# Two hybrid token-mixer layers in three-product float32r on one core: recurrence gates by blocks of 80 channels, rotated scores as stacked float32r products, another order of steps

## The chip, the cores and the metric

One Trainium2 chip, and of it one NeuronCore. The engines named below are TensorE (PE; PEld is its weight load), VectorE (DVE), ScalarE (ACT), GpSimd (POOL) and the sync engine (SP), which here issues nearly all DMAs. The metric is the time of one execution on the device in microseconds (us). It was measured three times for the kernel before; one more execution was recorded by the hardware profiler, and all rows of a trace come from that one.

## The reference, cut to what matters

Two layers run one after the other on x of 256 tokens by 1024 channels. Each projects the normalised x with one wide matrix and feeds three token mixers, whose outputs are gated, projected, merged and projected back:

```python
for l in range(DEPTH):                                   # DEPTH = 2
    h = rmsnorm(x, pre_norm_g[l])
    u, v, z_a, c_q, c_kv, k_rope, z_b, x_c, z_c, g_a, g_b, g_c = split(h @ w_in[l])
    y_a = gmlp_spatial(u, v, ...) * silu(z_a)            # spatial gating, 1024 channels
    y_b = mla_attention(c_q, c_kv, k_rope, ...) * silu(z_b)   # 8 heads
    y_c = rg_lru(x_c, ...) * silu(z_c)                   # recurrence, 1280 channels
    merged = (sigmoid(g_a) * (y_a @ w_proj_a[l]) + sigmoid(g_b) * (y_b @ w_proj_b[l])
              + sigmoid(g_c) * (y_c @ w_proj_c[l]))
    x = x + rmsnorm(merged @ w_out[l], post_norm_g[l])
```

Two places matter for the change. In the attention a head's score is a product over 128 plain channels plus a product over 64 rotated channels, whose key is shared by all heads. In `rg_lru` the gates come from block-diagonal matrices, 16 blocks of 80 by 80, with a bias:

```python
q, k = concat([q_nope, rope(q_rope)]), concat([k_nope, rope(k_rope)])    # 128 + 64
s = einsum('bqhd,bkhd->bhqk', q, k) * scale
...
xb = xc.reshape(B, S, 16, 80)                            # xc: causal conv of x_c
r = sigmoid(einsum('bshi,hij->bshj', xb, w_a).reshape(B, S, C) + b_a)
i = sigmoid(einsum('bshi,hij->bshj', xb, w_x).reshape(B, S, C) + b_x)
```

## The kernel before, in words

**Products.** A float32 operand is kept as two float32r tiles, a rounded high part (hi) and what is left (lo). `mm3` makes a product out of three matmuls, hi by hi, hi by lo and lo by hi (L307, L308, L309), so a 1024-deep projection onto 256 columns (`ch_mm`, one step of most keys) is 48 matmuls of 128x256. Scores, transposes and the value product of the attention use plain float32 tiles.

**Weights.** Each step of the list ORDER that needs weights has its own chunk, of 1 MB for most. A chunk is loaded by SP into one of three raw buffers (L200; the gates' pieces L210), split by ACT into hi (a copy, L268) and by DVE into lo (a subtraction, L269), and the split lands in one of three hi/lo pairs. When a step is through with its pair it hands it back: `done` puts the pair into the list and `pump` emits the split of the next chunk on ACT and DVE, then the load that the freed raw buffer takes. At which of a step's points that happens is set per key by LATE (`fin`). So ACT's and DVE's queues carry, in program order, a step's own work and the split of a chunk three ahead.

**Order.** Engines work through their instructions in the order in which the program emits them; that order is ORDER, written out by hand and used in both layers: steps for the low-rank queries and keys (xc, turn, conv, uq, ukv), the attention by pairs of heads (attend 0 to 5: scores of pair i, transposes of pair i-1, values of pair i-2), the spatial gating (v, norm, u, za), the merging gates (ga, gb, gc), their projections (pa, pb, pc), the output gates (zb, zc), and the recurrence (conv, split, stack, la, lx, r1, r2, r3).

**PSUM and temporaries.** `bank` is a ring of five PSUM banks (mm in the traces, mm_83 to mm_87 in the order), `aux` a ring of three, `tmp` a ring of eight 128x512 tiles in SBUF (t). A ring is taken in turn, so a step that takes a bank waits for the reader of what lay there five takes ago. Sixteen slots of SBUF hold the larger tiles.

**Recurrence gates.** The 1280 channels are two groups of five tiles of 128. Blocks of 80 cut across tiles of 128, so a gate chunk is 1280 columns of mostly zeros: POOL clears the raw buffer (L205), some 16 to 20 small DMAs lay the pieces (L210), and `lru_gate` multiplies in a mix of forms: 24 matmuls of 256 columns for each key (la, lx) and group, one in six of them with 96 rows (L927). The inputs that straddle tiles are gathered by `conv_stack` with copies on POOL, DVE and ACT (L447 is one of their lines). The bias enters in the sigmoid on ACT (L932), which writes the gates to SBUF, where `recur1` reads them: a multiply on DVE, five exponentials (L942) and five tanh (L944) on ACT, a square on DVE. `recur2` is two passes on DVE (L951, L952) and a square root on ACT (L953), `recur3` the scan.

**Scores.** `scores` makes four float32 products per head: the plain part at 128 and at 256 columns (L728, L730) and the rotated part at 128 and 256 columns (L729, L731). A plain float32 matmul is issued as two instructions (two passes), so the trace counts 32 for 16 heads. krt holds the rotated key twice, in rows 0 to 63 for one head of a pair and in rows 64 to 127 for the other, with zeros in the other half; qr holds a pair's rotated queries one above the other. The queries are rotated in `queries` (key uq): four copies on ACT (L643) and three operations on DVE (L646 is the second).

Of the kernel before, what the change touches and what calls it, by code (L numbers as in the profile page):

```python
# [7 lines left out]
F32 = mybir.dt.float32  # L8
# [5 lines left out]
P = 128  # L14
# [20 lines left out]
R_Q, R_KV, R_LG, R_LB, R_CW, R_CB, R_BA, R_BX, R_LAM, R_N = 0, 3, 5, 13, 21, 61, 71, 81, 91, 101  # L35
# [6 lines left out]
COL_EVEN, COL_ODD, COL_STACK, LRU_N = 0, GT * P, (GT + 2) * P, (GT + 5) * P  # L42


STACKS = ((0, ((1, 0, 32),)), (4, ((3, 96, 32),)), (2, ((1, 96, 32), (3, 0, 16))))
SH = 32
# [5 lines left out]
    ("wl", 0), ("xc", 0), ("turn", 0), ("xc", 1), ("conv", 0), ("uq", 0), ("conv", 1), ("xc", 2), ("ukv", 0),  # L52
    ("conv", 2), ("ukv", 1), ("decay", 0), ("ws", 0), ("xc", 3), ("uq", 1), ("attend", 0), ("shift", 0),
    ("uq", 2), ("v", 0),
    ("attend", 1), ("xc", 4), ("conv", 3), ("v", 1), ("conv", 4), ("uq", 3), ("attend", 2), ("split", 1),
    ("v", 2), ("v", 3), ("attend", 3), ("split", 0), ("norm", 0), ("u", 0), ("stack", 0), ("attend", 4),
# [9 lines left out]
LATE = {"ga": 1, "gb": 1, "lx": 1, "pa": 1, "ukv": 1, "uq": 3, "v": 1, "xc": 1}  # L66


SE = {
# [3 lines left out]
}  # L73

# [20 lines left out]
def tile_trunk(ctx: ExitStack, tc, I, out):  # L95
# [5 lines left out]
    sm = ctx.enter_context(tc.tile_pool(name="sm", bufs=2))  # L101
    psm = ctx.enter_context(tc.tile_pool(name="psm", bufs=1, space=bass.MemoryType.PSUM))
# [65 lines left out]
    for l in range(L):  # L168
# [4 lines left out]
        for key, j in ORDER:  # L173
            if key in COLS:
                c = Chunk(KT, CW, win(l, COLS[key] + j * CW))
            elif key == "uq":
                c = Chunk(3, 384, proj("mla_w_uq", l, 0, 3, j * 384, 384), kind="heads")
            elif key == "ukv":
                c = Chunk(2, 1024, proj("mla_w_ukv", l, 0, 2, j * 1024, 1024))
            elif key in ("la", "lx"):  # L180
                c = Chunk(LRU_N // P, P, lru=("lru_w_" + key[1], l, j))
# [12 lines left out]
    def load(c, parts=1, mid=None):  # L194
# [9 lines left out]
        name, l, g = c.lru  # L204
        G.memset(c.raw[:, :n], 0.0)  # L205

        def piece(row, col, r0, c0, nr, ncol):

            b = r0 // BW
            nc.sync.dma_start(  # L210
                c.raw[row : row + nr, col : col + ncol],
                I[name][l, g * 8 + b, r0 - b * BW : r0 - b * BW + nr, c0 - b * BW : c0 - b * BW + ncol],
            )

        for b in range(8):
            for k in range(GT):
                r0, r1 = max(b * BW, k * P), min(b * BW + BW, k * P + P)
                if r0 < r1 and k % 2 == 0:
                    piece(r0 - k * P, COL_EVEN + b * BW, r0, b * BW, r1 - r0, BW)
                elif r0 < r1:  # L220
                    c0, c1 = max(b * BW, k * P), min(b * BW + BW, k * P + P)
                    piece(r0 - k * P, COL_ODD + k // 2 * P + c0 - k * P, r0, c0, r1 - r0, c1 - c0)
        for n_, (m, runs) in enumerate(STACKS):
            for k, r, nr in runs:
                for b in range(8):
                    r0, r1 = max(b * BW, k * P + r), min(b * BW + BW, k * P + r + nr)
                    c0, c1 = max(b * BW, m * P), min(b * BW + BW, m * P + P)
                    if r0 < r1 and c0 < c1:
                        piece(r0 - k * P - r, COL_STACK + n_ * P + c0 - m * P, r0, c0, r1 - r0, c1 - c0)

    def split(c, parts=1, mid=None):
# [27 lines left out]
        if c.lru:  # L259
            act(hi[:, :n], c.raw[:, :n], AF.Copy)  # L260
            st = slice(COL_STACK, n)
            act(hi[SH : 2 * SH, st], c.raw[:SH, st], AF.Copy)
            V.tensor_tensor(lo[:, :COL_STACK], c.raw[:, :COL_STACK], f(hi[:, :COL_STACK]), ALU.subtract)
            V.tensor_tensor(hi[2 * SH : 3 * SH, st], c.raw[:SH, st], f(hi[:SH, st]), ALU.subtract)
            return
# [190 lines left out]
    with tc.manual_schedule():  # L456
# [10 lines left out]
        for i in range(2):  # L467
            G.memset(krt[i], 0.0)
# [62 lines left out]
        for l in range(L):  # L531
# [62 lines left out]
            def turn_ranks(_):  # L594
                for b in range(3):
# [9 lines left out]
                    for i in range(2):  # L605
# [15 lines left out]
            qr = slot("qr", (4, S))  # L621
# [5 lines left out]
            def queries(j):  # L627
# [68 lines left out]
            def conv_split(g):  # L696
                xh, xl = slot("xh", (GT, S), F32R), slot("xl", (GT, S), F32R)
                split_act(xh, xl, xc[g])
                cv[g] = xc[g], xh, xl

            def conv_stack(g):

                _, xh, xl = cv[g]
                xs, two = slot("xs", (GT, S), F32R), xm
                for src, dst in ((xh, xs[:, 3:5]), (xl, two)):
                    copy(SE.get("wide", "V"), dst[:64], f(src[:64, 2:5:2]))
                    copy(SE.get("wide2", "A"), dst[64:], f(src[64:, 0:3:2]))
                for n, (_, runs) in enumerate(STACKS):
                    for p, src in enumerate((xh, xl, xh)):
                        at = p * SH  # L710
                        for k, r, nr in runs:
                            copy(SE.get(("thin", n, p), "V"), xs[at : at + nr, n], f(src[r : r + nr, k]))
                cv[g] += (xs, two)

            cv = {}
# [397 lines left out]
```

## Time and profile before

| | |
|---|---|
| three executions | 797.0, 799.04, 799.51 us, median 799.04 |
| the profiled execution | 798.34 us, of it 796.6 us span of the trace |
| PE | 788.1 us busy, 99% of the span |
| DVE | 548.9 us, 69% |
| ACT | 469.3 us, 59% |
| POOL | 70.5 us, 9% |
| DMA | 137.87 MB, 173 GB/s on the mean |

The span runs from the first to the last recorded instruction; 1.74 us of the profiled execution lie around it. A group row of the profile reads: line, engine, operation, written tile <- read tiles, shape, count | total us, mean ns of one | idle time of the engine ahead of it and what ended it. Matmul durations in group rows overlap (a matmul is in the pipe for longer than it holds it), so what a matmul costs is read from the distance between starts in the timeline, or from the chain that ended last, whose rows add up to the span.

### The profile page before, as it was taken

What the parts mean: (1) busy time and instruction counts of PE and PEld (TensorE: products, weight loads), DVE (VectorE), ACT (ScalarE), POOL (GpSimd) and SP (SyncE); (2) the same over time, 40 slices, a digit from 0 to 9 for tenths busy, and PEclk for the clock granted to TensorE, in tenths of its full rate; (3) what the DMA queues carried; (4) which work ended last, traced back from release to release, by engine and by line L of the source; (5) the groups of instructions that cost most, each with busy time, mean ns of one, the idle gap of its engine ahead of it and who ended that gap; (6) DMA issues with size and microseconds to landing.
All of it is one profiled execution on the core that took longest, in us unless ns stands there. A gap on an engine that the chain in (4) does not pass through costs nothing.

```text
span 796.6 us, 15355 instructions
## 1 busy us (share of the span) xinstructions
PE 788.1 (99%) x6445; PEld 780.2 (98%) x6445; DVE 548.9 (69%) x712; ACT 469.3 (59%) x689; POOL 70.5 (9%) x110
## 2 busy tenths in 40 slices
PE   9999999999999999999999999999999999999996
PEld 8999999999999999999999999999999999999996
DVE  5587788666876787555666868776578578775562
ACT  5785767339855736343567776654595584544441
POOL 1100503003000000000010032031210000000000
PEclk9999999999999999999999999999999999999998
DMA  7845454344666565666357626541575656564531
GB/s 229 290 152 182 153 161 155 112 122 137 201 213 211 159 215 169 199 212 216 109 171 239 208 94 211 159 128 51 166 219 167 221 162 202 185 214 150 193 132 54
DMA packets 134205, 137.87 MB, mean 173 GB/s; under 512 B 11046, under 2 KB 130808, under 8 KB 134136
## 3 DMA queue, kind: packets, MB, share of 16 engines
q1 hardware_dynamic: 134120, 136.90, 54.3%
q8 instruction: 50, 0.82, 0.4%
q14 instruction: 19, 0.16, 0.1%
q10 hardware_dynamic: 16, 0.00, 0.0%
HBM read 135.83 MB, written 1.05 MB: 172 GB/s over the span
## 4 chain that ended last, share of the span: by engine, by line
PE 94%; DMA 2%; issue 1%; DVE 1%; ACT 1%; SPq 0%; POOL 0%; POOLq 0%; DVEq 0%; ACTq 0%
PE mm L308 25%; PE mm L307 25%; PE mm L309 25%; PE mm L431 2%; PE mm L433 2%; PE mm L432 2%; DMA raw<-in_w_in_dram 1%; PE aux L843 1%; PE mm L730 1%; PE aux L770 1%; PE mm L731 1%; DMA X<-in_x_dram 1%; PE mm L549 1%; PE aux L1021 1%; PE mm L1020 1%
## 5 line engine op out<-in xcount | busy, mean ns | idle before, releaser
L269 DVE TENSOR_TENSOR wlo<-raw,whi 128x2048 fp32r<-128x2048 f32 (+5 forms) x123 | 264.6, 2156 | 115.9 <-ACT whi L268 115.5
L307 PE MATMUL mm<-hT,whi 128*128 128x256 f32 x1088 | 307.1, 282 | 0.0
L309 PE MATMUL mm<-hT,wlo 128*128 128x256 f32 x1088 | 305.8, 281 | 0.3 <-DVE wlo L269 0.3
L308 PE MATMUL mm<-hT,whi 128*128 128x256 f32 x1088 | 305.6, 281 | 0.0
L268 ACT ACTIVATE whi<-raw 128x2048 fp32r<-128x2048 f32 (+5 forms) x123 | 221.0, 1802 | 66.6 <-PE mm L308 26.8
L309 PEld LDWEIGHTS mm<-hT,wlo 128*128 128x128 f32 x1088 | 205.0, 188 | 0.5 <-DVE wlo L269 0.5
L307 PEld LDWEIGHTS mm<-hT,whi 128*128 128x128 f32 x1088 | 205.0, 188 | 0.0
L308 PEld LDWEIGHTS mm<-hT,whi 128*128 128x128 f32 x1088 | 205.0, 188 | 0.0
L973 ACT ACTIVATE t<-mm 128x512 f32<-128x512 f32 x18 | 10.8, 598 | 52.2 <-PE mm L309 52.2
L397 POOL TENSOR_TENSOR rstd<-rstd,mhalf 128x1 f32<-128x1 f32 x8 | 4.4, 551 | 391.1 <-DVE rstd L396 391.1
L308 PE MATMUL mm<-yc,whi 128*128 128x256 f32 x128 | 36.0, 282 | 0.0
L308 PE MATMUL mm<-ya,whi 128*128 128x256 f32 x128 | 36.0, 282 | 0.0
L307 PE MATMUL mm<-ya,whi 128*128 128x256 f32 x128 | 36.0, 281 | 0.0
L307 PE MATMUL mm<-yc,whi 128*128 128x256 f32 x128 | 36.0, 281 | 0.0
L431 PE MATMUL mm<-whi,hT 128*128 128x256 f32 x128 | 36.0, 281 | 0.0
L308 PE MATMUL mm<-yb,whi 128*128 128x256 f32 x128 | 35.9, 281 | 0.0
L309 PE MATMUL mm<-ya,wlo 128*128 128x256 f32 x128 | 35.9, 280 | 0.0
L309 PE MATMUL mm<-yc,wlo 128*128 128x256 f32 x128 | 35.9, 280 | 0.0
L309 PE MATMUL mm<-yb,wlo 128*128 128x256 f32 x128 | 35.8, 280 | 0.0
L307 PE MATMUL mm<-yb,whi 128*128 128x256 f32 x128 | 35.8, 280 | 0.0
L432 PE MATMUL mm<-wlo,hT 128*128 128x256 f32 x128 | 35.8, 279 | 0.0
L433 PE MATMUL mm<-whi,hT 128*128 128x256 f32 x128 | 35.7, 279 | 0.0
(279 smaller groups left out, 1663.4 us busy)
## 6 DMA issues: line engine op xcount, KB each, us to landing
raw<-in_w_in_dram SPq DMA_DIRECT2D x76, 1024.0 KB
raw<-in_w_proj_a_dram SPq DMA_DIRECT2D x8, 1024.0 KB
raw<-in_w_proj_b_dram SPq DMA_DIRECT2D x8, 1024.0 KB
raw<-in_w_proj_c_dram SPq DMA_DIRECT2D x8, 1024.0 KB
raw<-in_w_out_dram SPq DMA_DIRECT2D x8, 1024.0 KB
raw<-in_mla_w_uq_dram SPq DMA_DIRECT2D x8, 576.0 KB
raw<-in_mla_w_ukv_dram SPq DMA_DIRECT2D x4, 1024.0 KB
raw<-in_w_in_dram SPq DMA_DIRECT2D x4, 640.0 KB
```

The source lines that it names most:

```text
L268: act(hi[:, w], c.raw[:, w], AF.Copy)
L269: V.tensor_tensor(lo[:, w], c.raw[:, w], f(hi[:, w]), ALU.subtract)
L307: mm(ps, lh, rh, start=start, stop=False)
L308: mm(ps, lh, rl, start=False, stop=False)
L309: mm(ps, ll, rh, start=False, stop=stop)
L431: mm(ps, lh, rh, start=k == 0, stop=False)
L432: mm(ps, lh, rl, start=False, stop=False)
L433: mm(ps, ll, rh, start=False, stop=k == KT - 1)
L549: mm(ps, ll, rh, start=False, stop=j % 2 * 4 + k == KT - 1)
L730: mm(sc[:, P : 3 * P], qn[:, P:], kn, start=True, stop=False)
L731: mm(sc[:, P : 3 * P], qp[:, P:], kr, start=False, stop=True)
L973: act(sg, ps, AF.Sigmoid)
```

## The change

**Gates by blocks.** A key's chunk is now `lg`, for four blocks (h = 0 to 3) and both gates. The stacked input is 80 hi rows, a row of ones and 47 lo rows (128 deep), and a second one 80 hi rows, one of ones and the other 33 lo rows (114 deep); the stacked weights are hi weights with the bias as row 80, and hi again for the lo rows, against lo weights. So a block needs two matmuls of 256 columns instead of a mix of forms, and a step `lg` is 16 matmuls into four banks with 80 output rows each. Four sigmoids of 80x512 without bias follow, and each result is stored to DRAM (L908 in the new numbering); `gate_in` (key in, L915) reads the gates of a group back in the layout of 128 channels to a tile. The conv output's hi and lo parts go to DRAM too (L687), and `conv_stack` reads them back as blocks (L698, L699), two slots for each h, after POOL has set rows 64 to 95 to one. The clearing of raw buffers, the small pieces, the gathering copies, the bias columns and their transposed rows are gone.

**Scores.** krt and qr become float32r: krt0 is the rotated key's hi part in both halves, krt1 its lo part, and qr holds for every head its hi rows above its lo rows (or below, for the second of a pair). A head's rotated part is two float32r matmuls in one pass each at 128 columns, and two at 256, in place of one float32 matmul (two passes) at each. Every uq step gets two copies on ACT and two subtractions on DVE of 64x256, after its pump.

**Order.** ORDER is another one, and LATE holds `lg` at 1 in place of `lx`.

```diff
 ORDER = (
...
-    ("za", 0), ("u", 1), ("za", 1), ("attend", 5), ("u", 2), ("za", 2), ("u", 3), ("za", 3), ("ga", 0),
-    ("la", 0), ("lx", 0), ("r1", 0), ("stack", 1), ("pa", 0), ("ga", 1), ("pa", 1), ("la", 1), ("r2", 0),
...
+    ("za", 2), ("u", 3), ("stack", 1), ("conv", 4), ("za", 3), ("attend", 5), ("conv", 3), ("lg", 0), ("ga", 0),
+    ("split", 1), ("pa", 0), ("ga", 1), ("lg", 1), ("in", 0), ("pa", 1), ("ga", 2), ("stack", 2), ("pa", 2),
+    ("r1", 0), ("stack", 3), ("ga", 3), ("r2", 0), ("pa", 3), ("zb", 0), ("r3", 0), ("lg", 2), ("zb", 1),
+    ("zb", 2), ("zb", 3), ("lg", 3), ("gb", 0), ("pb", 0), ("in", 1), ("gb", 1), ("pb", 1), ("r1", 1), ("r2", 1),
...
-LATE = {"ga": 1, "gb": 1, "lx": 1, "pa": 1, "ukv": 1, "uq": 3, "v": 1, "xc": 1}
+LATE = {"ga": 1, "gb": 1, "lg": 1, "pa": 1, "ukv": 1, "uq": 3, "v": 1, "xc": 1}
...
-        G.memset(c.raw[:, :n], 0.0)
...
+        l, g = c.lru
+        for i, x in enumerate("ax"):
+            at = slice(i * WH, (i + 1) * WH)
+            w = I["lru_w_" + x][l, g * NH : (g + 1) * NH].rearrange("b r c -> r b c")
+            r1, r2 = v2(c.raw[:, at], BW), v2(c.raw[:, W2 + i * WH : W2 + (i + 1) * WH], BW)
+            nc.sync.dma_start(r1[:BW], w)
+            nc.sync.dma_start(r1[B1:], w[:K1])
+            nc.sync.dma_start(c.raw[BW:B1, at], I["lru_b_" + x][l : l + 1, g * WH : (g + 1) * WH])
+            nc.sync.dma_start(r2[64 : B1 + K2], w[K1 - (B1 - 64) :])
...
-            act(hi[:, :n], c.raw[:, :n], AF.Copy)
...
+            raw, r2 = c.raw[:, :W2], c.raw[64 : B1 + K2, W2 : 2 * W2]
+            act(hi[:, :W2], raw, AF.Copy)
+            act(lo[64 : B1 + K2, :W2], r2, AF.Copy)
+            V.tensor_tensor(lo[:B1, :W2], raw[:B1], f(hi[:B1, :W2]), ALU.subtract)
...
+                for a in range(2):
+                    own, other = (slice(i * HR, (i + 1) * HR) for i in (a, 1 - a))
+                    to = qr[j // 2][:, j % 2 * 2 + a]
+                    act(to[own], qa[own, :S], AF.Copy)
+                    V.tensor_tensor(to[other], qa[own, :S], f(to[own]), ALU.subtract)
...
+                    d = dp.tile([GT * P, S], F32, tag=f"{w}{g}", name=nm(w))
+                    nc.sync.dma_start(d.rearrange("(k p) s -> p k s", p=P), f(x))
...
+            def conv_stack(h):
+                _, _, dh, _, dl = cv[h // 2]
+                rows = slice(h % 2 * WH, (h % 2 + 1) * WH)
+                bh, bl = (d[rows].rearrange("(b r) s -> r b s", r=BW) for d in (dh, dl))
+                st2[h] = [slot("xs", (NH, S), F32R) for _ in range(2)]
+                for x, b in zip(st2[h], (bl[:K1], bl[K1:])):
+                    G.memset(f(x[64:96]), 1.0)
+                    nc.sync.dma_start(f(x[:BW]), bh)
+                    nc.sync.dma_start(f(x[B1 : B1 + b.shape[0]]), b)
...
-                    mm(sc[:, 0:P], qp[:, 0:P], kr[:, 0:P], start=False, stop=True)
...
-                    mm(sc[:, P : 3 * P], qp[:, P:], kr, start=False, stop=True)
...
+                    for o, ts, n in ((sc[:, 0:P], slice(0, P), P), (sc[:, P : 3 * P], slice(P, S), S)):
+                        mm(o, qn[:, ts], kn[:, :n], start=True, stop=False)
+                        mm(o, qp[:, ts], krt[0][:, :n], start=False, stop=False)
+                        mm(o, qp[:, ts], krt[1][:, :n], start=False, stop=True)
...
+            def lru_gates(h):
...
+                    for b0 in range(0, NH, 2):
+                        ps, o = bank(), tmp()
+                        for b in (b0, b0 + 1):
+                            ws = slice(i * WH + b * BW, i * WH + (b + 1) * BW)
+                            pb = ps[:BW, (b - b0) * S : (b - b0 + 1) * S]
+                            mm(pb, wh[:, ws], x1[:, b], start=True, stop=False)
+                            mm(pb, wl[: B1 + K2, ws], x2[: B1 + K2, b], start=False, stop=True)
+                        act(o[:BW], ps[:BW], AF.Sigmoid)
+                        nc.sync.dma_start(rows[:, b0 : b0 + 2], v2(o[:BW], S))
+                fin(c, "lg", 1)
+
+            def gate_in(g):
+                for key in ("la", "lx"):
+                    o = slot(key, (GT, S))
+                    nc.sync.dma_start(o, gates[key, g].rearrange("(k p) s -> p k s", p=P))
+                    gates[key, g] = o
```

The first place is ACT's queue around the step ga 1 of the first layer. In the order of before, whi is a chunk's hi part written by the split, t_80 is ga 1's gate (a sigmoid, L875) and la the recurrence gate of group 1, with its bias from pt:

```order
L260 ACTIVATE whi_92<-raw_89 128x1280
L262 ACTIVATE whi_92<-raw_89 32x384
L268 ACTIVATE whi_94<-raw_90 128x2048
L875 ACT_TABLE_LOAD
L875 ACTIVATE t_80<-mm_84 128x512
L268 ACTIVATE whi_96<-raw_91 128x2048
L932 ACTIVATE la_2268<-mm_81,pt_349 128x256 x2
L932 ACTIVATE la_2268<-mm_82,pt_349 128x256 x2
```

In the changed kernel the same place reads as follows (L243 is the split's copy, L860 the gate's sigmoid, L907 that of the recurrence gates):

```order
L243 ACTIVATE whi_98<-raw_93 128x2048
L243 ACTIVATE whi_94<-raw_91 128x2048
L860 ACTIVATE t_78<-mm_86 128x512
L907 ACTIVATE t_79<-mm_87 80x512
L907 ACTIVATE t_80<-mm_83 80x512
L907 ACTIVATE t_81<-mm_84 80x512
L907 ACTIVATE t_82<-mm_85 80x512
L243 ACTIVATE whi_96<-raw_92 128x2048
```

The step after ga 1 is lg 1 now, not pa 1, and lg 1 takes four banks (mm_87, 83, 84, 85) after the one of ga 1 (mm_86); pa 1, which follows, takes the fifth, mm_86.

The second place is ACT's queue at the recurrence of group 0. Of before (a, la and u are tiles of the recurrence, xs the stacked inputs of group 1):

```order
L942 ACT_TABLE_LOAD
L942 ACTIVATE a_2079<-la_2013,sA_777 128x256 x5
L944 ACTIVATE la_2013<-la_2013,sT_776 128x256 x5
L447 ACTIVATE xs_2093<-xl_1255 32x256 x3
L447 ACTIVATE xs_2093<-xl_1255 16x256
L447 ACTIVATE xs_2093<-xh_1254 32x256
L447 ACTIVATE xs_2093<-xh_1254 16x256
L260 ACTIVATE whi_92<-raw_89 128x1280
```

Of the changed kernel (L923 and L925 are the exponentials and tanh, L934 the root, L954 the sigmoid of zb 0, and t_76 the gate of ga 3):

```order
L923 ACTIVATE a_2351<-la_2176,sA_743 128x256 x5
L925 ACTIVATE la_2176<-la_2176,sT_742 128x256 x5
L237 ACTIVATE whi_98<-raw_93 128x640
L238 ACTIVATE wlo_99<-raw_93 50x640
L860 ACT_TABLE_LOAD
L860 ACTIVATE t_76<-mm_84 128x512
L934 ACT_TABLE_LOAD
L934 ACTIVATE u_2352<-u_2352 128x1280
L243 ACTIVATE whi_94<-raw_91 128x2048
L954 ACT_TABLE_LOAD
L954 ACTIVATE t_77<-mm_86 128x512
```

The root, which stood behind the gates of group 1, now follows the exponentials with one gate of ga 3 between, and the sigmoid of zb 0 stands behind both and behind a split.

The third place is SP's queue at the step ga 1. Of before there are only weights (raw):

```order
L210 DMA raw_91<-in_lru_w_x_dram 16x64 x2
L200 DMA raw_89<-in_w_proj_a_dram 128x8x256
L200 DMA raw_90<-in_w_in_dram 128x8x256
L200 DMA raw_91<-in_w_proj_a_dram 128x8x256
L210 DMA raw_89<-in_lru_w_a_dram 80x80
```

Of the changed kernel (la_1955 and lx_1968 are the gates in DRAM, la_2176 and lx_2178 those in SBUF; L201 to L205 are the pieces of an lg chunk):

```order
L192 DMA raw_91<-in_w_proj_a_dram 128x8x256
L908 DMA la_1955<-t_79 80x2x256
L908 DMA la_1955<-t_80 80x2x256
L908 DMA lx_1968<-t_81 80x2x256
L908 DMA lx_1968<-t_82 80x2x256
L192 DMA raw_92<-in_w_in_dram 128x8x256
L915 DMA la_2176<-la_1955 128x5x256
L915 DMA lx_2178<-lx_1968 128x5x256
L201 DMA raw_93<-in_lru_w_a_dram 80x4x80
```

Stores of the gates, a load of weights, and the reads of the gates now stand in one queue, in this order.

More of the change, by code (lines that the diff above doesn't have):

```diff
@@ L32 @@
 CWID = 4
[L35 to L46, printed above, removed]
+R_Q, R_KV, R_LG, R_LB, R_CW, R_CB, R_LAM, R_N = 0, 3, 5, 13, 21, 61, 71, 81
+NH, K1 = 4, 47
+K2 = BW - K1
+WH = NH * BW
+W2 = 2 * WH
+B1 = BW + 1
 SLOT_W = 1296
 ORDER = (
[L52 to L56, printed above, removed]
[6 rows of a table removed]
-)
-LATE = {"ga": 1, "gb": 1, "lx": 1, "pa": 1, "ukv": 1, "uq": 3, "v": 1, "xc": 1}
-SE = {
[3 rows of a table removed]
-}
[10 rows of a table added]
+)
+LATE = {"ga": 1, "gb": 1, "lg": 1, "pa": 1, "ukv": 1, "uq": 3, "v": 1, "xc": 1}
 class Chunk:
@@ L101, in tile_trunk @@
     sm = ctx.enter_context(tc.tile_pool(name="sm", bufs=2))
+    dp = ctx.enter_context(tc.tile_pool(name="dp", bufs=1, space=bass.MemoryType.DRAM))
     psm = ctx.enter_context(tc.tile_pool(name="psm", bufs=1, space=bass.MemoryType.PSUM))
@@ L179, in tile_trunk @@
                 c = Chunk(2, 1024, proj("mla_w_ukv", l, 0, 2, j * 1024, 1024))
[L180 to L181 removed]
+            elif key == "lg":
+                c = Chunk(2 * NH, 2 * BW, lru=(l, j))
             elif key in ("pa", "pb", "pc"):
@@ L203, in load @@
             return
-        name, l, g = c.lru
-        G.memset(c.raw[:, :n], 0.0)
[L207 to L229, printed above, removed]
+        l, g = c.lru
[7 more added lines that the diff above has]
+            nc.sync.dma_start(r2[64 : B1 + K2], w[K1 - (B1 - 64) :])
     def split(c, parts=1, mid=None):
@@ L318, in tile_trunk @@
     sinK = const.tile([P, NT, 64], F32, name="sinK")
-    krt = [const.tile([P, S], F32, name=f"krt{i}") for i in range(2)]
+    krt = [const.tile([P, S], F32R, name=f"krt{i}") for i in range(2)]
     hT = [const.tile([P, NT, KT, P], F32R, name=f"hT{i}") for i in range(2)]
     X = const.tile([P, NT, D], F32, name="X")
-    xm = const.tile([P, 2, S], F32R, name="xm")
     def layer_consts(l, rows):
@@ L620, in tile_trunk @@
             vv = [slot("vv", (D,)) for _ in range(NT)]
-            qr = slot("qr", (4, S))
+            qr = [slot("qr", (4, S), F32R) for _ in range(2)]
             xp = [slot("xp", (GT, S + 3)) for _ in range(2)]
@@ L696, in conv_split @@
             def conv_split(g):
[L697 to L715, printed above, removed]
+                cv[g] = [xc[g]]
+                for w in ("xh", "xl"):
+                    x = slot(w, (GT, S), F32R)
+                    if w == "xh":
+                        act(x, xc[g], AF.Copy)
+                    else:
+                        V.tensor_tensor(x, xc[g], f(cv[g][1]), ALU.subtract)
+                    d = dp.tile([GT * P, S], F32, tag=f"{w}{g}", name=nm(w))
+                    nc.sync.dma_start(d.rearrange("(k p) s -> p k s", p=P), f(x))
+                    cv[g] += [x, d]
+            def conv_stack(h):
[7 more added lines that the diff above has]
+                    nc.sync.dma_start(f(x[B1 : B1 + b.shape[0]]), b)
+            cv, st2 = {}, {}
             oT = [slot("oT", (4, S)) for _ in range(2)]
@@ new lines, in lru_gates @@
+            def lru_gates(h):
+                x1, x2 = st2[h]
+                c = get(l, "lg", h)
+                wh, wl = (t.rearrange("p a b -> p (a b)") for t in (c.hi, c.lo))
+                for i, key in enumerate(("la", "lx")):
+                    if h % 2 == 0:
+                        gates[key, h // 2] = dp.tile([GT * P, S], F32, tag=f"{key}{h // 2}", name=nm(key))
+                    rows = gates[key, h // 2][h % 2 * WH : (h % 2 + 1) * WH].rearrange("(b r) s -> r b s", r=BW)
+                    for b0 in range(0, NH, 2):
[8 more added lines that the diff above has]
+                fin(c, "lg", 1)
```

49 lines of the change are left out of this document (7 added, 42 removed), and 13 rows, old and new, of tables (ORDER, SE).

## The prediction

> **What bounds the kernel now.** I read the page's busy times first, then PE's waits, then the chain that ended last for what the attention's matmuls cost, then stretches of the timeline at the places that the new order touches. The page:
>
> ```profile
> span 796.6 us, 15355 instructions
> ...
> PE 788.1 (99%) x6445; PEld 780.2 (98%) x6445; DVE 548.9 (69%) x712; ACT 469.3 (59%) x689; POOL 70.5 (9%) x110
> ...
> PEclk9999999999999999999999999999999999999998
> ...
> GB/s 229 290 152 182 153 161 155 112 122 137 201 213 211 159 215 169 199 212 216 109 171 239 208 94 211 159 128 51 166 219 167 221 162 202 185 214 150 193 132 54
> ...
> q1 hardware_dynamic: 134120, 136.90, 54.3%
> ```
>
> PE is busy from end to end at the full granted clock, and all its waits together are these:
>
> ```profile
> PE aux L479 <- POOL ones L457: 1.0, 1, 1.0
> PE mm L549 <- DVE hT L505: 0.5, 1, 0.5
> PE mm L309 <- DVE wlo L269: 0.3, 1, 0.3
> ```
>
> That is 1.8 us in three places. So the time is the sum of the matmuls. A change gains what it takes off PE's list, less the waits that it makes; work on DVE, ACT, POOL or the queues counts only where it makes PE wait. There is next to nothing to win from removed waits, and a great deal to lose from new ones.
>
> **Gates: fewer matmuls.** In PE's timeline one key of group 1 (24 matmuls) stands between these two starts; the second row is the first matmul of the step behind it:
>
> ```profile
> 202.02 0.28 PE L307 MATMUL mm<-xh,whi 128*128 128x256 f32 x1
> ...
> 204.88 0.29 PE L307 MATMUL mm<-hT,whi 128*128 128x256 f32 x1
> ```
>
> 2.86 us for 24 is 0.119 us from start to start. Before there are 2 layers x 2 groups x 2 keys x 24 = 192 such matmuls, after 2 layers x 4 steps x 16 = 128, at 256 columns too. 64 fewer at 0.119 are **-7.6 us**. The new ones have 80 output rows and 128 or 114 rows deep; the 24 hold four with 96 rows at the same pace, so I take no other price. With 0.119, a step of 48 matmuls is 5.7 us and a step lg 1.9 us; both are used below.
>
> **Scores: one float32 matmul becomes two float32r ones.** The chain has a pair's matmuls, one float32 matmul being two instructions, and other widths for comparison (L667 is a float32r matmul at 512 columns, L759 six transposes in one pass at 128):
>
> ```profile
> 53.27 0.23 PE mm L667
> ...
> 71.04 0.22 PE mm L728 x2
> 71.26 0.22 PE mm L729 x2
> 71.48 0.43 PE mm L730 x2
> 71.92 0.43 PE mm L731 x2
> ...
> 85.92 0.65 PE aux L759 x6
> ```
>
> The rotated part is L729 and L731: 0.22 + 0.43 = 0.65 us a head, 10.4 us for 16 heads. After, each head has two float32r matmuls at 256 columns, 0.119 each, and two at 128, whose price x no row shows. Its bounds: on a line through 256 (0.119) and 512 columns (0.23), 128 would cost 0.064; the dearest row at 128 is the whole float32 matmul, 0.22. With the first, 16 x 2 x (0.064 + 0.119) = 5.9, a gain of 4.5; with the second 10.8, a loss of 0.4. I take the row that is nearest in form, one pass at 128 columns: 0.65 / 6 = 0.108, and L728 halved is 0.11. Then 16 x 2 x (0.108 + 0.119) = 7.3, **-3.1 us**.
>
> [...]
>
> **New wait, lg 1 to pa 1.** The five banks are taken in turn, and lg takes four, so pa 1 writes the bank that ga 1's sigmoid reads. PE reaches pa 1 one lg, 1.9 us, after the end of ga 1. The sigmoid stands on ACT behind the copy of the split that ga 1 has just released. That pair elsewhere in the trace, on ACT:
>
> ```profile
> 287.73 1.91 ACT L268 ACTIVATE whi<-raw 128x2048 fp32r<-128x2048 f32 x1
> 289.54 0.57 ACT L875 ACTIVATE t<-mm 128x512 f32<-128x512 f32 x1
> ```
>
> From the copy's start to the sigmoid's end are 2.38 us; less 1.9 leaves 0.5, and I take 0.6 with the handing over: **+1.2 us** in two layers. The bounds are 0 and the copy once more (1.9 a layer, 3.8 in all), if ACT is a split behind. Behind the waiting matmul stands all of PE's list, so it counts in full.
>
> **New wait, zb 1.** Two places later zb 1 takes the bank of zb 0 (lg 2 lies between with four). zb 0's bank is free when DVE has multiplied it by its sigmoid, and on ACT this sigmoid stands behind the exponentials, the tanh, ga 3's gate and the square root. ACT's timeline of before at r1, group 1 of the second layer:
>
> ```profile
> 645.65 1.28 ACT L942 ACT_TABLE_LOAD   x1
> 646.94 2.12 ACT L942 ACTIVATE a<-la,sA 128x256 f32<-128x256 f32 x5
> 648.97 2.10 ACT L944 ACTIVATE la<-la,sT 128x256 f32<-128x256 f32 x5
> ```
>
> and the groups of what follows them:
>
> ```profile
> L269 DVE TENSOR_TENSOR wlo<-raw,whi 128x2048 fp32r<-128x2048 f32 x108 | 248.0, 2299 | 112.4 <-ACT whi L268 112.2
> L268 ACT ACTIVATE whi<-raw 128x2048 fp32r<-128x2048 f32 x108 | 206.7, 1915 | 60.7 <-PE mm L308 26.8 <-issue 26.3 <-DMA raw<-in_w_in_dram 3.0
> L875 ACT ACTIVATE t<-mm 128x512 f32<-128x512 f32 x24 | 14.2, 590 | 19.3 <-PE mm L309 19.2
> L974 DVE TENSOR_TENSOR t<-mm,t 128x512 f32<-128x512 f32 x18 | 12.4, 686 | 18.7 <-ACT t L973 18.7
> L897 DVE TENSOR_TENSOR acc<-t,mm 128x512 f32<-128x512 f32 x8 | 5.5, 681 | 0.1
> L951 DVE SCALAR_TENSOR_TENSOR u<-u,la 128x1280 f32<-128x1280 f32 x4 | 5.9, 1483 | 0.0
> L952 DVE TENSOR_SCALAR u<-u 128x1280 f32<-128x1280 f32 x4 | 3.3, 827 | 0.1
> L953 ACT ACTIVATE u<-u 128x1280 f32<-128x1280 f32 x4 | 5.1, 1274 | 14.8 <-DVE u L952 14.8
> ```
>
> PE needs the bank 3 x 5.7 + 1.9 = 19.0 us after pa 2's end (ga 3, pa 3, zb 0, lg 2). The longest way to it: split copy of pa 2 1.9; table 1.3, exponentials and tanh 4.2; lg 2's split copies some 1.2 (two of 640 columns, by L268's pace, from 1915 ns for 2048); table 1.3 and gate 0.6; DVE's two passes 2.3, partly behind the gate; table 1.3 and root 1.3; split copy 1.9 with its subtraction 2.3, in part beside the next table and sigmoid (1.9); acc 0.7 and the multiply 0.7. All that in a row but the overlaps (the gate and its table beside DVE's passes, table and sigmoid beside the subtraction) comes to 19.1 to 19.3. I take 0.2 a layer, **+0.4**, with bounds 0 and 3 in all. Cover and need are nearly equal, so every further delay on ACT at this place is PE's.
>
> **New wait, attend 0.** The rotated queries of uq 0 now need two copies and two subtractions more before the scores of pair 0 (64x256; nearest rows here):
>
> ```profile
> L643 ACT ACTIVATE t<-mm 32x256 f32<-32x256 f32 x32 | 12.0, 376 | 0.8 <-PE mm L309 0.3
> L638 ACT ACTIVATE q<-mm 128x512 f32<-128x512 f32 x8 | 4.9, 612 | 0.0
> L646 DVE TENSOR_TENSOR t<-t,sinT 128x256 f32<-128x256 f32 x8 | 3.4, 430 | 0.0
> ```
>
> After uq 0, PE has uq 1, ws and uq 2: 27 + 27 matmuls and four transposes, 6.8 us. The chain is 0.6 + 4 x 0.38 + 3 x 0.43, then the split's copy (1.9; it is emitted ahead of the new operations), then 2 x 0.38 + 0.43: 6.5, and the split's subtraction on DVE can push it over. I take 0.5 a layer, **+1.0**, bounds 0 and 3. The rest of these operations, 6.0 us of ACT and 6.9 of DVE over 8 steps, lie beside PE.
>
> **DRAM traffic.** Each layer adds the stores of hi and lo (4 x 0.655 = 2.6 MB), the stacks' reads (four times 240 rows of 4 KB, 3.9 MB) and the gates' stores and reads (2.6 each): 11.8 MB, so 160 MB in all, 201 GB/s on the mean. From queue 1's share, 136.9 MB / (0.543 x 796.6 us) = 316 GB/s is my estimate of what the engines carry when always busy. The stage where the change sits, of before:
>
> ```profile
> core 0: us, PE busy (x) PEld busy (x) DVE busy (x) ACT busy (x) POOL busy (x), PEclk, DMA share, GB/s
> 165.00:240.00 75.00, 75.00 (x636) 75.00 (x636) 52.12 (x49) 53.08 (x70) 8.74 (x9) 1.00 0.58 179
> ...
> ```
>
> After, the stretch from lg 0 to pa 3 (49 us) holds eight chunks of 1.05 MB, two of lg and 5.9 MB of the new traffic, about 15 MB: 305 GB/s, nearly all that the estimate allows. What hides it is lead. The tightest new path is group 0's gates: lg 1's last sigmoid comes 3.1 us after lg 1's end (1.9 + 0.6 + 4 x 0.6 - 1.9, rounded up), then a store and a read, each at most a megabyte's trip in company:
>
> ```profile
> 16.95 7.41 DMA raw<-in_w_in_dram
> ```
>
> 3.1 + 2 x 7.4 = 17.9, and ACT wants them 3 x 5.7 + 1.9 + 1.3 = 20.3 us after lg 1. So I cost it at nothing, with 2.4 us to spare. The gathering copies, POOL's clearing, the bias rows and the small pieces that go away were hidden and bring nothing.
>
> **Sum.** 798.34 - 7.6 - 3.1 + 1.2 + 0.4 + 1.0 = 790.2 us against the profiled execution. That lies 0.7 under the median of the runs, 799.04, so the median I predict is **790.9**.
>
> **Rivals.** *Float32r at 128 columns costs what float32 does* (x about 0.22): the score part brings nothing, 794.4. For it: L729's time with two passes is no proof of what one float32r pass takes; against it: the transposes' 0.108. Chance 0.19. *It costs less*, 0.064 by the line through the wider rows: 16 x 2 x 0.044 = 1.4 more, 789.5; the fall from 0.23 to 0.119 speaks for it, the transposes against. Chance 0.1.
>
> *Waits eat the gain*: the three waits reach their bounds (3.8 + 3 + 3 = 9.8 instead of 2.6), 798.1. For it: at all three places ACT's queue is as long as what PE has in front of it. Against it: ACT is 59% busy, DVE 69%, and before such backlogs made PE wait 0.3 us in all. Chance 0.13.
>
> *Slower, by the gates' way through DRAM.* ACT works in order: if the gates are late at r1, the splits behind wait too. A pair's split has two steps, 11.4 us, for a copy and a subtraction (4.2) and the step's own three operations (0.6 + 0.7 + 0.7), so 5 us to spare. With a trip of T, PE waits 3.1 + 2T - 20.3 - 5 = 2T - 22.2 us at each of four recurrences. The gain of 8.1 and 2.4 us of measurement are used up at T = 12.4. With a store behind one load in flight and a read behind two (3.3 us each by 316 GB/s) the trips are 10.7 and 14.0, mean 12.4; with 14.0 for both it is 23 us. So it decides at about 801, and I put it at 806. For it: 305 of 316 GB/s, and SP's queue, where reads wait for stores and loads stand behind the reads. Against it: slices of 290 GB/s already run without a wait on PE, and a store of gates is 0.16 MB. [...] Chance 0.13.
>
> **How the numbers follow.** Forecast 0.45, dear 128 columns 0.19, cheap ones 0.1, waits 0.13, DRAM 0.13. About 0.3% (2.4 us) is what a measurement here can tell from no change: faster 0.74, same 0.13, slower 0.13. The range begins at the cheapest prices with no new wait (798.34 - 7.6 - 4.5 = 786.2, and 0.7 to the median) and reaches over the first rivals to the waits' case at 798.8: 786.5 to 799.5 leaves out the DRAM rival and little else.
>
> **What would show it.** In the changed profile: PE's waits name ga 1's sigmoid before pa 1 and the multiply before zb 1 with under a microsecond each; 16 matmuls of lg take 1.9 us; two score matmuls at 128 columns take 0.22 together. I am wrong if PE's busy time does not fall by about 10 us, or if its waits exceed 8 us, above all on the splits behind r1 or on stacked inputs from DRAM.

## The result, and the profile after

The changed kernel took 849.38 us (median of 848.8 to 852.81) against 799.04: the ratio is 1.0644, 95% interval 1.061 to 1.0678. It is slower by 50 us, where 790.9 us and a range of 786.5 to 799.5 were predicted. The profiled execution took 852.81 us.

The page after:

```profile
span 851.0 us, 15278 instructions
...
PE 794.6 (93%) x6381; PEld 783.5 (92%) x6381; DVE 543.1 (64%) x708; ACT 465.5 (55%) x673; POOL 61.4 (7%) x92
...
PEclk9999999997978999999999999999989879999999
DMA  7845555559545966855456646546795389566531
...
q1 hardware_dynamic: 162056, 162.47, 60.8%
```

PE now has gaps of 56 us in all (851.0 - 794.6), and its clock is below full speed in the slices around the recurrence gates of both layers (down to 7 tenths in the PEclk row), so the matmuls that do run there are slower too (those of pa against whi at L282 have 295 ns in the mean, at L307 before 281): PE's busy time has risen by 6.5 us although there are 64 instructions fewer on it. PE's waits (us in total, times, longest):

```profile
PE mm L905 <- DVE acc L882: 12.2, 2, 6.1
PE mm L905 <- DMA xs<-xl: 9.2, 2, 4.8
PE mm L282 <- ACT whi L243: 8.6, 2, 4.3
PE mm L282 <- DVE t L955: 6.9, 2, 3.6
PE mm L906 <- DMA xs<-xl: 4.8, 4, 1.5
PE mm L284 <- DVE wlo L244: 3.1, 2, 1.5
PE mm L282 <- ACT t L860: 2.3, 2, 1.4
```

Each comes twice or so, once a layer. Only 14.0 us name a transfer, that of the stacked lo rows (xs<-xl); the rest names ACT and DVE, which must have been late for a reason of their own. ACT's waits give it:

```profile
ACT whi L243 <- DMA raw<-in_w_in_dram: 69.0, 17, 11.1
...
ACT whi L243 <- DMA raw<-in_w_proj_a_dram: 23.5, 2, 11.8
```

ACT's splits stand for 92 us waiting for weights. In the kernel before the same view has one such row, of 8.9 us:

```profile
ACT whi L268 <- DMA raw<-in_w_in_dram: 8.9, 4, 3.2
```

So the loads are late. One would look for a full DMA system next. The stretch from 206 to 286 us of both kernels, before and after, in that order (the steps in it are not quite the same ones; the last two columns are the DMA share and GB/s, the one ahead of them the granted clock):

```profile
206.00:286.00 80.00, 80.00 (x678) 80.00 (x678) 60.57 (x54) 49.89 (x52) 1.21 (x2) 1.00 0.62 195
```

```profile
206.00:286.00 80.00, 64.73 (x485) 63.55 (x485) 41.15 (x37) 40.27 (x47) 2.01 (x3) 0.87 0.64 191
```

On the mean the DMA engines are hardly busier here than before, 0.64 against 0.62, and PE loses 15 of 80 us. (In the 60 us ahead of this stretch the share rose from 0.47 to 0.68, and PE lost 8.5 us.) What is late is late without the DMA system being full on the mean. SP's timeline in the changed kernel has the first trace of the cause, in the time that an issue takes:

```profile
173.83 0.36 SPq L201 DMA_DIRECT2D raw<-in_lru_w_x_dram  x1
174.23 0.32 SPq L202 DMA_DIRECT2D raw<-in_lru_w_x_dram  x1
174.59 2.68 SPq L203 DMA_DIRECT2D raw<-in_lru_b_x_dram  x1
177.32 0.28 SPq L205 DMA_DIRECT2D raw<-in_lru_w_x_dram  x1
177.70 0.32 SPq L698 DMA_DIRECT2D xs<-xh  x1
178.06 0.31 SPq L699 DMA_DIRECT2D xs<-xl  x1
178.47 5.25 SPq L698 DMA_DIRECT2D xs<-xh  x1
```

An issue takes 0.3 us, but that of a bias row (L203, 1.2 KB) behind a transfer of 47 rows (L202) takes 2.7 us here. All 16 bias rows of the trace are held like this, for 2.2 to 5.9 us each and 59 us together, and what they wait for by their semaphores had ended some 4 us or more before they start. The 5.25 us of the last line are only in part of this kind: this read waits for POOL to set its rows to one, which is done at 181.86, and 1.9 us are left after that. The longest issue of a stack's hi rows is 8.6 us, and there the trace shows no such wait. The chain that ended last (start, us, what) goes through long issues and through the loads behind them:

```profile
151.17 5.13 SPq L203
...
157.45 2.66 SPq L203
...
160.54 5.56 DMA raw<-in_w_in_dram
166.20 1.93 ACT whi L243
...
185.40 3.80 SPq L908
...
191.64 8.84 DMA raw<-in_w_in_dram
...
236.70 11.19 DMA raw<-in_w_in_dram
...
252.06 11.19 DMA raw<-in_w_in_dram
```

Weight loads of 9 us and more are no proof by themselves: the versions e1 and e3 below, which lose nothing, have them too (the longest load of 1 MB takes 13.7 and 12.3 us there and 12.5 here, the medians are 5.7, 5.8 and 6.1). What these two do not have is the held issues, behind which the weights are issued late, and stacked inputs that land as late.

The completion counts in the traces say why: how many steps a DMA's semaphore takes goes by the rows of the transfer. By rows, in the changed kernel, from issue to landing (worked out from the trace's semaphore records; the time of a held issue is part of it):

```
rows  KB    steps of the semaphore   us to landing: least, median, most
128   1024  16                       5.0   6.1  12.5   (weights)
 80   320   16                       3.4  11.9  17.2   (stack, hi rows)
 47   188    2                      11.5  14.5  17.5   (stack, lo rows)
 33   132   12                       8.7   9.1   9.3   (stack, lo rows)
 47    59    2                       4.7   5.3   9.3   (gate weights)
 50    62   11                       2.5   2.6   2.7   (gate weights)
```

In the traces of both kernels, before and after, transfers of 16, 32, 48, 64, 80 and 128 rows have 16 steps. Those of 1, 2, 3, 8, 10, 33, 40, 47 and 50 rows have 2, 3, 4, 9, 11, 12, 11, 2 and 11: the largest divisor up to 16, and one more, which comes 0.09 to 0.21 us after the end of the issue. So for 47 rows a single step tells of the data. The packets agree. Where a 47-row transfer alone is under way, one packet moves at a time: from 159.5 to 160.5 us (a weights' piece) and from 181.2 to 182.0 us (a stack's rows) the DMA share is 0.07, at 19 and 23 GB/s, while from 145 to 146 us, with loads of 128 rows, it is 1.10, at 364 GB/s (a packet's time overlaps that of the next a little). That is one engine of 16. Of a 50-row piece at most ten packets move at a time, in the eight pieces with no transfer close behind. For the other counts the number of engines is the author's reading of the steps; which engine it is, no run here shows.

The transfers behind such a one are late by a single step; that this is the step of the engine they share with it is the author's reading. The 80-row read issued at 178.47 has fifteen of its 16 steps 7.7 to 8.4 us after the issue and the last after 13.7; the weights issued at 184.90 have fifteen after 5.3 to 6.5 us and the last after 10.6. Over the 16 reads of 80 rows the last step comes 3.9 us behind the fifteenth in the median, in e3 0.1. And a bias row, whose semaphore takes two steps too, lands 0.18 to 0.19 us behind the 47 rows ahead of it, all 16 times. In the kernel before, the pieces of the gate weights had 16 to 80 rows, all in multiples of 16, and its trace held nothing of this.

### The profile page after: what moved, and what is told of

Read it like the earlier page. It is cut to its first block, busy times and chain, and to the rows that moved or that the text cites. A ratio compares the mean times of both kernels' runs of the same rounds, so it can differ in the third digit from the quotient of the medians.

```text
span 851.0 us, 15278 instructions
## 1 busy us (share of the span) xinstructions
PE 794.6 (93%) x6381; PEld 783.5 (92%) x6381; DVE 543.1 (64%) x708; ACT 465.5 (55%) x673; POOL 61.4 (7%) x92
## 4 chain that ended last, share of the span: by engine, by line
PE 71%; DMA 10%; SPq 7%; DVE 6%; issue 3%; ACT 2%; POOL 1%; DVEq 0%; POOLq 0%; ACTq 0%
PE mm L282 18%; PE mm L283 17%; PE mm L284 17%; DMA raw<-in_w_in_dram 8%; SPq L698 3%; DVE wlo L244 2%; SPq L203 2%; ACT whi L243 2%; PE mm L406 2%; PE mm L407 2%; PE mm L405 2%; PE mm L714 1%; DMA raw<-in_w_proj_a_dram 1%; DVE xc L672 1%; PE mm L521 1%
## 5 line engine op out<-in xcount | busy, mean ns | idle before, releaser
L282 PE MATMUL mm<-hT,whi 128*128 128x256 f32 x1088 | 310.6, 285 | 15.5 <-ACT whi L243 8.6
L243 ACT ACTIVATE whi<-raw 128x2048 fp32r<-128x2048 f32 (+5 forms) x123 | 220.9, 1802 | 157.6 <-DMA raw<-in_w_in_dram 69.0
L282 PEld LDWEIGHTS mm<-hT,whi 128*128 128x128 f32 x1088 | 209.2, 192 | 16.9 <-ACT whi L243 9.0
L284 PEld LDWEIGHTS mm<-hT,wlo 128*128 128x128 f32 x1088 | 208.8, 192 | 3.7 <-DVE wlo L244 3.7
L283 PEld LDWEIGHTS mm<-hT,whi 128*128 128x128 f32 x1088 | 209.1, 192 | 0.5 <-issue 0.5
L905 PE MATMUL mm<-xs,whi 128*80 128x256 f32 x64 | 19.7, 330 | 22.1 <-DVE acc L882 12.2
L282 PE MATMUL mm<-ya,whi 128*128 128x256 f32 x128 | 37.7, 295 | 2.3 <-ACT t L860 2.3
L283 PE MATMUL mm<-ya,whi 128*128 128x256 f32 x128 | 37.2, 290 | 0.0
L282 PE MATMUL mm<-yb,whi 128*128 128x256 f32 x128 | 36.0, 281 | 0.0
L282 PE MATMUL mm<-yc,whi 128*128 128x256 f32 x128 | 35.9, 281 | 0.0
```

The source lines that it names most:

```text
L243: act(hi[:, w], c.raw[:, w], AF.Copy)
L282: mm(ps, lh, rh, start=start, stop=False)
L283: mm(ps, lh, rl, start=False, stop=False)
L284: mm(ps, ll, rh, start=False, stop=stop)
L905: mm(pb, wh[:, ws], x1[:, b], start=True, stop=False)
```

## The experiments

Theory A, one engine: transfers of 47 rows fill one of 16 engines, and all that follows in SP's queue waits for its share on it. Theory B, the total: traffic of the stage or the trips through DRAM. Theory C, SP: too many issues. All times are medians, with the ratio to the kernel before on the same chip:

| kernel | us | ratio, 95% interval |
|---|---|---|
| changed kernel | 849.38 | 1.0644 (1.061 to 1.0678) |
| e1: 47 rows as 32 + 15 | 786.55 | 0.9849 (0.9834 to 0.9863) |
| e2: the same, stacks only | 802.72 | 1.0046 (1.003 to 1.0062) |
| e3: 45 + 35 lo rows | 786.15 | 0.9846 (0.9819 to 0.9873) |
| e4: stacks' lo rows by POOL's queue | 822.1 | 1.0305 (1.028 to 1.0331) |
| e5: before, u loads cut at row 47 | 813.2 | 1.0178 (1.0163 to 1.0194) |
| e6: before, u loads cut at row 48 | 797.55 | 0.9986 (0.9977 to 0.9996) |
| e7: e3 with plain rotated scores | 788.59 | 0.9878 (0.9854 to 0.9902) |
| e8: 46 + 34 lo rows | 820.37 | 1.0272 (1.0254 to 1.029) |
| e9: e3 with the buffers at their old places | 789.88 | 0.9888 (0.9871 to 0.9904) |

**e1, the 47 rows in two.** The edit:

```diff
-            nc.sync.dma_start(r1[B1:], w[:K1])
+            nc.sync.dma_start(r1[B1 : B1 + 32], w[:32])
+            nc.sync.dma_start(r1[B1 + 32 :], w[32:K1])
...
-                    nc.sync.dma_start(f(x[B1 : B1 + b.shape[0]]), b)
+                    n = 32 if b.shape[0] == K1 else b.shape[0]
+                    nc.sync.dma_start(f(x[B1 : B1 + n]), b[:n])
+                    if n < b.shape[0]:
+                        nc.sync.dma_start(f(x[B1 + n : B1 + K1]), b[n:])
```

> Every transfer of 47 rows (the stacks' reads, 188 KB, and the gate weights' pieces, 59 KB) is cut into 32 + 15 rows; bytes, order of work and queue stay. Theory A (in the changed kernel's trace a transfer of 80 or 128 rows is landed by 16 engines, one of 33 rows by 11, one of 47 rows by a single one, so the 47-row transfers fill one of the 16 DMA engines, and every later load waits for its share on that engine): PE's waits fall from about 50 us to under 10 us, the granted clock goes back to 0.99 or more, and the time is 788 to 800 us. Theory B (the stage's total traffic of about 200 GB/s, or the two trips through DRAM, is what is too slow): bytes and trips are the same, so 840 us or more. Theory C (SP issues too many DMAs, one after the other): there are more of them, so 849 us or more.

786.55 us: the whole loss is gone, with more DMAs and the same bytes (the time lies 1.5 us under the expected range). B and C fall. The stretch from 206 to 286 us moves more bytes in e1 than in either kernel, with a DMA share of 0.90, and PE loses 1.2 of 80 us in it:

```profile
206.00:286.00 80.00, 78.83 (x668) 78.38 (x668) 55.61 (x47) 55.63 (x66) 2.01 (x3) 1.00 0.90 259
```

The page of e1, and the two waits that are left at the gates:

```profile
span 786.2 us, 15306 instructions
...
PE 774.6 (99%) x6381; PEld 767.0 (98%) x6381; DVE 542.8 (69%) x708; ACT 465.4 (59%) x673; POOL 62.2 (8%) x92
...
PEclk9999999999999999999999999999999999999998
...
GB/s 224 288 156 186 166 158 201 208 162 323 251 267 260 331 169 209 272 156 182 126 197 218 167 150 156 209 190 183 198 350 249 235 305 274 212 169 188 259 59 54
```

```profile
PE mm L283 <- ACT t L864: 0.9, 2, 0.5
PE mm L283 <- DVE t L959: 0.6, 1, 0.6
```

PE is at 99% and at full clock again. The slices at the gates reach 331 and 350 GB/s, which is more than the 316 that the prediction took for the engines' limit.

**e2, only the stacks.** The second half of e1's edit alone.

> Only the stacks' 47-row reads are cut into 32 + 15 rows; the gate weights' 47-row pieces stay. Theory A: the stacks' reads have 4 x 188 KB a layer on the one engine, the weights' pieces 8 x 59 KB, so most of the loss goes: 795 to 815 us, with SP still held for 2 to 5 us at each bias piece behind the weights' pieces. Theory B: 840 us or more.

802.72 us. Of the 62.8 us between the changed kernel and e1, cutting the stacks' reads alone brings 46.7, and the weights' pieces, cut as well, the other 16.2. The 16 bias rows behind those pieces still take SP 54.5 us to issue. What is left on PE is waits for late splits and for what stands on ACT and DVE behind them:

```profile
PE mm L282 <- DVE t L958: 6.8, 2, 3.6
PE mm L284 <- DVE wlo L244: 3.5, 3, 1.4
```

**e3, one number.** 45 lo rows in the first stack and 35 in the second make the same sum of products.

```diff
-NH, K1 = 4, 47
+NH, K1 = 4, 45
...
-            nc.sync.dma_start(r1[B1:], w[:K1])
+            nc.sync.dma_start(r1[B1 : B1 + K1], w[:K1])
...
-                            mm(pb, wh[:, ws], x1[:, b], start=True, stop=False)
+                            mm(pb, wh[: B1 + K1, ws], x1[: B1 + K1, b], start=True, stop=False)
```

(The split takes the same 126 rows.)

> The same products, stacked as 45 + 35 lo rows and not 47 + 33: 45 rows divide over 15 engines, 35 over 7, the second weight piece has 52 rows (13 engines). One number changes, the count of DMAs does not. Theory A: like the version with 32 + 15 rows, within 4 us of it (35 rows on 7 engines may cost a little). Theories B and C: 840 us or more, since neither bytes, trips nor count change.

786.15 us, with as many DMAs as the changed kernel. The semaphores of the 45 rows step 16 times, of the 35 rows 8 times, and the same issues on SP as shown above are short:

```profile
168.62 0.39 SPq L201 DMA_DIRECT2D raw<-in_lru_w_x_dram  x1
169.05 0.47 SPq L202 DMA_DIRECT2D raw<-in_lru_w_x_dram  x1
169.56 0.27 SPq L203 DMA_DIRECT2D raw<-in_lru_b_x_dram  x1
169.88 0.31 SPq L205 DMA_DIRECT2D raw<-in_lru_w_x_dram  x1
170.28 0.33 SPq L698 DMA_DIRECT2D xs<-xh  x1
170.66 0.46 SPq L699 DMA_DIRECT2D xs<-xl  x1
171.22 0.35 SPq L698 DMA_DIRECT2D xs<-xh  x1
```

The stacks' lo rows land after 5.5 us in the median (45 rows, 180 KB) against 14.5 (47 rows, 188 KB), and the hi rows after 5.9 against 11.9; the 16 bias rows take SP 4.6 us to issue against 59. This and e1 are the fastest versions; e7 and e9, which build on this one, beat both kernels too.

**e4, another queue.**

```diff
-                    nc.sync.dma_start(f(x[B1 : B1 + b.shape[0]]), b)
+                    nc.gpsimd.dma_start(f(x[B1 : B1 + b.shape[0]]), b)
```

> The 47-row and 33-row reads of the stacks are issued by POOL on a queue of its own, and stay 47 and 33 rows. Theory A, if the engine is the limit: it still has 188 KB to move for each read and shares its time between two queues, so some of the loss stays: 805 to 845 us. Theory D (the order in SP's one queue is what makes the loads late, not the engine): near the version with 32 + 15 rows, under 803 us. If POOL's queue spreads the rows over the engines in another way than SP's, that shows as a landing by more engines and also gives under 803 us.

822.1 us. Theory D falls as the only cause: out of SP's queue the 47-row reads land no earlier (16.8 us in the median), and 36 us of the loss stay. But 27 us come back, so what these reads hold up in SP's queue is a part of it. On POOL's queue the semaphore takes 16 steps for 47 rows as well, so there the count doesn't set them apart; but fifteen of them come early and the last 5.3 to 9.4 us behind the fifteenth, so a single step is late there too. The weights' pieces stay on SP in this kernel; by e2 they make 16 of these 36.

**e5 and e6, the cost put into the kernel before.** Half of each u chunk's load is cut by rows, at 47 in e5 and at 48 in e6 (c.cut is true for the four u chunks of a layer):

```diff
+            if c.cut:
+                for r, k in ((slice(0, 47), slice(0, 4)), (slice(47, P), slice(0, 4)), (slice(0, P), slice(4, 8))):
+                    nc.sync.dma_start(raw[r, k], src[r, k])
+                return
```

> The kernel before, with nothing changed but the loads of the four u chunks of each layer: half of each (k tiles 0 to 3, 4 KB a row) is issued as rows 0 to 46 and rows 47 to 127, the other half as one transfer. Theory A: the 47 rows, 188 KB, go to one engine, which at a sixteenth of my 316 GB/s takes 9 to 10 us; the loads behind lose that much of a lead of 7 to 14 us, eight times, so the time is 3 to 30 us over the version with rows cut at 48, and PE waits on splits in the stage of u and za. Theories B and C: the same as cut at 48.

> The same cut at row 48 (48 and 80 rows, both 16 engines): bytes and number of DMAs as with the cut at 47. Theory A: no slower than the kernel before by more than 0.3%, 797 to 801 us. Theory C (number of DMAs on SP): as slow as the cut at 47.

813.2 and 797.55 us: one row moved from one transfer to the other costs 15.7 us in eight loads, in a kernel that has no gates by blocks, no trip through DRAM and the old order. The 47 rows land after 14.6 us in the median, the 48 rows after 3.1; the 512 KB behind them, 128 rows in both, after 10.6 and 4.9. (The rest of that half has 81 rows in e5 and 80 in e6; what part of the difference is its, no run shows.) PE waits in e5 for a softmax that stands on ACT and DVE behind a late split, and not in e6 (the expectation had the splits of u and za themselves):

```profile
PE aux L766 <- DVE t L758: 9.7, 2, 5.2
```

The chain of e5 that leads to this split has a held issue (L204 issues the cut loads) and the load behind it:

```profile
103.35 9.14 SPq L204
...
112.54 10.44 DMA raw<-in_w_in_dram
```

Two more DMAs for a chunk cost nothing (e6): theory C has no share in it.

**e7, the scores alone.** e3 with one float32 matmul in place of two float32r ones in the rotated part:

```diff
-                        mm(o, qp[:, ts], krt[0][:, :n], start=False, stop=False)
-                        mm(o, qp[:, ts], krt[1][:, :n], start=False, stop=True)
+                        mm(o, qp[:, ts], krt[a][:, :n], start=False, stop=True)
```

> The version with 45 + 35 rows, its rotated scores put back to one plain float32 product each (and the split of the rotated queries and keys with it). If the score part is worth what the trace's distances between starts say (20.9 us before, 17.8 after), this is 3.1 us slower than the version with 45 + 35 rows: about 789.3 us. If the gain there only moved elsewhere (ACT and DVE have fewer operations now), it is within 1 us of it.

788.59 us, 2.4 more than e3. The single times of both spread by 4 to 5 us, so the median alone doesn't settle the size; in the traces the distances between starts of all score matmuls add up to 20.6 us here and 17.8 in e3.

**e8, the divisor or the odd number.** K1 = 46 in e3's code.

> One number: 46 + 34 lo rows. By the rule that the traces so far fit (rows go to as many engines as the largest divisor up to 16: 47 to 1, 33 to 11, 45 to 15, 35 to 7), 46 and 34 rows go to 2 engines each, and the second weight piece, 51 rows, to 3. Theory A: the hot engines have a little over half of what the one had with 47 rows, so a part of the loss comes back: 793 to 830 us, between 45 and 47 rows. A rival within A (odd or prime counts are what is slow, not the divisor): as with 45 rows, 784 to 790 us.

820.37 us, with even counts: the semaphores of 46 and 34 rows step three times, of 51 rows four times. So it is not the odd count: 46 and 34 are even, and their largest divisor up to 16 is 2. The two kinds of stack reads now land after 9.3 and 10.9 us in the median, and the splits are late again:

```profile
PE mm L282 <- ACT whi L243: 8.8, 2, 4.4
PE mm L905 <- DVE acc L882: 5.0, 2, 2.8
PE mm L284 <- DVE wlo L244: 4.3, 3, 1.8
```

**e9, where the buffers lie.** PE's busy time in e3 is 773.1 us, 15.0 under the kernel before, where the prediction had 10.7 for gates and scores. e9 gives the constants' area the bytes back that the change took from it, so that the weight buffers lie where they lay:

```diff
+    xm = const.tile([P, 2, S], F32, name="xm")
+        G.memset(xm[:, 0, :2], 0.0)
-        pt = const.tile([P, R_N], F32, tag="pt", name=nm("pt"))
+        pt = const.tile([P, 101], F32, tag="pt", name=nm("pt"))
```

> The version with 45 + 35 rows is some 4 us faster than the fewer matmuls and the waits explain: the three-product matmuls that read the normalised input (tile hT) as moving operand stand 116.8 ns apart there and 118.3 in the kernel before, those that read it as stationary operand 118.2 against 116.7. The change also freed 2 KB and 80 bytes of each partition ahead of all weight buffers. Here those bytes are taken again (a tile of 512 floats of which two are written, and the table of columns at its old width), nothing else. If the place of the weight buffers in SBUF sets the distance, it is back at 118.3 and 116.7 ns and the time is 3 to 5 us over the version with 45 + 35 rows, about 790 us. If other work of the changed kernel (fewer copies on POOL, DVE and ACT) sets it, distance and time stay: 116.8 ns, 784 to 788 us.

789.88 us. PE's line of the page of e3, and then of e9:

```profile
PE 773.1 (99%) x6381; PEld 765.9 (98%) x6381; DVE 542.8 (69%) x708; ACT 464.9 (59%) x673; POOL 62.0 (8%) x92
```

```profile
PE 778.1 (99%) x6381; PEld 771.2 (98%) x6381; DVE 543.1 (69%) x708; ACT 464.7 (59%) x673; POOL 61.0 (8%) x93
```

The same list takes 5.0 us more. The matmuls that read hT as moving operand against whi stand 118.4 ns apart in e9 and 116.8 in e3, those that have hT as stationary operand 116.9 and 118.2: both are back at the values of before. So the place of the buffers gives the 4 to 5 us. What about the place does it (a bank, an alignment) was not tried.

## Why the prediction was wrong

The step that failed is the one on DRAM traffic: "So I cost it at nothing, with 2.4 us to spare." It tested two things: the bytes of the stage against the rate of 16 engines (305 of an estimated 316 GB/s), and the lead of the gates' store and read, each at the 7.41 us of a load of 1 MB in 128 rows. The stacks' reads stood in it as bytes alone and the gate weights' pieces not at all, and no transfer was priced by its rows. A 47-row read of 188 KB took 11.5 to 17.5 us, more than that megabyte, and what queued behind it was late as well. From e3 to the changed kernel the spans differ by 851.0 - 782.6 = 68.4 us: 46.9 of it is PE's idle time (56.4 against 9.5) and 21.5 its busy time (794.6 against 773.1, the same instructions at the lower clock). The second part was not in the prediction at all. In the changed kernel's trace the clock is at half in eight stretches of 3.4 to 10.2 us around the gates, 58 us in all; in e3, where PE waits little, there is none there.

The prediction's own signs of being wrong did show: PE's busy time rose by 6.5 us in place of falling by about 10, and PE waits 14.0 us for stacked inputs from DRAM. (One of its sums is off: the waits' case is 798.1 with the 0.7 to the median in it, and the range, which ends by 798.8, counts the 0.7 again. Nothing here hangs on it.)

The rival that came out slower had the sign and, in part, the way (late loads, late splits), but not the mechanism: it needed the gates' store and read to take over 12.4 us a trip. In the changed kernel they took 6.1 to 6.6 and 6.2 to 7.8 in the median (10.6 and 9.4 at most), about the 7.4 assumed, and no wait in its trace names them; in e8 ACT and DVE wait 5.4 us for the reads, PE in no run. What it had right is that loads stand behind reads in SP's queue (27 us by e4), but the reads were the stacks', with the gate weights' pieces beside them. The total of 305 GB/s was no limit either (331 and 350 in slices of e1).

The other terms stood, as e1, e3 and e9 show without the narrow transfers:

- *Gates, -7.6.* A matmul of lg stands 0.120 us from the next in e3; 128 of them are 15.4 against 22.8 before, -7.4.
- *Scores, -3.1.* All score matmuls together take 20.9 us before and 17.8 after, -3.1. The single prices differ from the assumed ones (0.112 for the second float32r matmul at 128 columns, up to 0.3 where a float32r one follows a float32 one at 256), but the sum is the same.
- *lg 1 to pa 1, +1.2.* The row of e1 has 0.9 us in two times.
- *zb 1, +0.4.* 0.6 in e1, once.
- *attend 0, +1.0.* No such wait is in e1 or e3; the cover was enough.
- Not foreseen: the 4 to 5 us by the buffers' place.

With the old places and no narrow transfers (e9) the time is 789.88 us, where the sum gave 790.9: PE's busy time is 10.0 us under that of before for the 10.7 of the sum, and its gaps are 0.6 us longer for 2.6. So the reading of PE held, and one price on the DMA side, taken by bytes, turned the sign. What the other order is worth by itself, no run shows.

## What to carry to other kernels

Before costing a transfer by its bytes, count the rows of its outermost dimension: here 47 rows moved at a DMA share of 0.07, one engine of 16, and landed after 14.5 us in the median, 45 rows after 5.5. Cut the rows into counts that were quick here (32 + 15 in e1, 48 and 80 in e6), or choose the split of the work so that such counts come out (45 + 35 for 47 + 33 cost nothing here and was worth 63 us). When splits or loads are late while the DMA share is no higher than before, look in SP's timeline for issues of 2 to 6 us that no semaphore explains, and at how many steps the completion semaphores take and how late the last one comes; and where a kernel is at 99% of PE, count with lost clock besides the waits (21.5 us beside 46.9 here).

## What the runs showed of the hardware that was not expected

- One row less in a transfer (47 for 48, in eight loads) made its landing 14.6 us for 3.1, and 15.7 us of the kernel.
- An issue on SP behind a transfer of 47 rows was held (2.2 to 5.9 us for 0.3 at the bias rows), and with it all later issues of that queue; what holds it inside the queue is not shown. A second queue did not help the narrow transfer itself (16.8 us against 14.5).
- The granted clock over the 80 us with PE at 81% (64.73 of 80) was 0.87.
- The same matmuls are 1.5 ns of 118 closer together or further apart by where their operands lie, 5.0 us over the kernel.
